# Value projection of the second row block: f32r parts replaced by scaled f16 high and low parts, with a new order of its banks

## The chip, the cores and the metric

The kernel runs on one core of one Trainium2 chip, in one launch. The metric is device microseconds of that core. The kernel before took 448.49 us, the median of three runs (447.81 to 448.59).

## What is computed

One layer of a hybrid bidirectional encoder over 1024 tokens of width 1024, in float32. A combined projection gives the queries, keys, values and gates of two head groups; group A attends in a 2-D neighbourhood of a 16 x 64 token grid, group B in a band of 128 tokens with rotary positions and a sink logit; each output is multiplied by SiLU of its gate, projected, added to the scaled input and normalised.

```python
h = jnp.einsum('bsd,de->bse', x, w_in[layer])
q_a, k_a, v_a, z_a, q_b, k_b, v_b, z_b = jnp.split(h, SPLIT_POINTS, axis=-1)
y_a = neighborhood_attention(q_a..., k_a..., v_a..., rel_pos_bias[layer])
y_b = windowed_gqa_with_sink(rotary(q_b), rotary(k_b), v_b..., sink_logits[layer])
mixed = jnp.concatenate([y_a * jax.nn.silu(z_a), y_b * jax.nn.silu(z_b)], axis=-1)
x = layer_norm(DEEPNORM_ALPHA * x + jnp.einsum('bse,ed->bsd', mixed, w_out[layer]), ...)
```

The change lies in the part of the first line that gives the values v_a (512 columns) and v_b (128 columns), 640 columns of W_in together.

## The kernel before

Float32 accuracy is had from parts of lower precision: an operand is split into a high part and a low part (what is left), and three matmuls are added up in PSUM, high x high, low x high and high x low. The tokens are dealt with in two row blocks (`half` 0 and 1) of 512 tokens; the inner dimension of 1024 is cut into KT = 8 slices k of 128.

The kernel opens with the value projection (L434 to L606), whose instructions are in an order written out by hand (`manual_schedule`, L548): each engine runs its own instructions in program order, and waits only for data and for buffers.

**First row block** (L549 to L564). Eight PSUM banks hold four token tiles t of 128 times two column halves a of 320. `load_wv(k)` (L457) loads 128 x 640 of the weights to `wvraw` (three buffers), ACT casts the high part `wvh` (L467), DVE subtracts for the low part `wvl` (L470), both in f32r. `load_x(half, k)` (L445) does the same for 128 x 512 of x transposed, by way of `xraw` (four buffers), giving `xh` and `xl`. The loop over k runs two slices of loads ahead of the matmuls; per k, 24 matmuls (`v_mms`, L478, L483) of 320 columns, with x stationary, go round the eight banks. From k = 4 on (`X1AT`) two slices of the second block's x are loaded and split beside it. `x_max` (L490) takes the maximum of |x| of each of the 16 slices on DVE.

**What is queued behind it** (L565 to L573): on SP's queue, five weight tiles of the later projections (`w_load`), ten loads of x once more (`x2_load`, L516), mask, sink and rotary tables. ACT empties the eight banks to `v32` (`v_out`, L539).

**Second row block** (L581 to L604). Bank by bank, i = 0 to 7, each with its 24 matmuls over k. Threaded into it: the scale of x (`x_scale`, L504: PE transposes the row maxima, DVE makes the power-of-two scale `xsc`), the scans of the first four weight tiles on ACT (`w_scan`, L234), sums of those on DVE (`z_tree`, L239 to L241), the scales of the first two projections (`w_scale`, L243: a small matmul into a bank with tag t, L249, and five small DVE operations), and the f16 parts of x, both halves, for the later projections (`x16_part`, L521): high on ACT (L529), low on DVE (L534) or, for five of the 16, on POOL in two instructions (L531, L532). `w_split(m)` (L196) makes the f16 parts of a weight tile: high on ACT (L204), low on POOL (L209, L210), and asks SP for the tile five further on. `v_max` (L543) takes the maximum of each token tile's values.

**After it** the projections `project(name)` (L379) run in f16, 48 matmuls of 512 columns each at L402. `v_scale` (L610), 16 matmuls into the first of them, needs all eight maxima; `v_part` (L623) writes the values' f16 parts to DRAM. The remaining weight tiles come through `sum_load` (L639) into tiles of the pool `big`. From L1185 on attention units are threaded between the rest of the projections, and `final` (L1053) ends with the output projection and the normalisation.

PSUM has eight banks under three tags: pj (2), s (4), t (2). `bank(tag)` hands one out; a matmul into a bank waits until the one that had it has been read. Tiles with one tag in an SBUF pool share its buffers in the same way.

Of the kernel before, what the change touches and what calls it, by code (L numbers as in the profile page):

```python
# [17 lines left out]
HD = 64  # L18
# [48 lines left out]
def hybrid_block(ctx, tc, xT, x, wt, wv, wo, bias, sink, gain, lbias, cos, sin, bmask, out):  # L67
# [4 lines left out]
    big = ctx.enter_context(tc.tile_pool(name="big", bufs=8))  # L72
# [15 lines left out]
    def big_tile(name, shape=(128, 2, 512), dt=F32R):  # L88
        n = taken[0]
        taken[0] += 1  # L90
        tag = "big" if n < 8 or 16 <= n < 24 or n >= 32 + NS else "big2"
        return big.tile(list(shape), dt, tag=tag, name=name)

    xh, xl, x16h, x16l = {}, {}, {}, {}
    for half in range(2):
        for k in range(KT):
            t = big_tile(f"x{half}{k}")
            xh[half, k], xl[half, k] = t[:, 0, :], t[:, 1, :]
# [335 lines left out]
    with ExitStack() as vctx:  # L434
# [10 lines left out]
        def load_x(half, k, cuts=(0, 512)):  # L445
            raw = vp.tile([128, 512], F32, tag="xr", name="xraw", bufs=4)
            for q, a, b in zip((nc.scalar, nc.sync) if len(cuts) == 3 else (nc.sync,), cuts, cuts[1:]):
                q.dma_start(raw[:, a:b], xT[half, k, :, a:b])
                yield
            for a, b in zip(cuts, cuts[1:]):  # L450
                (nc.scalar.copy if len(cuts) == 2 else nc.vector.tensor_copy)(xh[half, k][:, a:b], raw[:, a:b])
                yield
            for a, b in zip(cuts, cuts[1:]):
                nc.vector.tensor_sub(xl[half, k][:, a:b], raw[:, a:b], xh[half, k][:, a:b].bitcast(F32))
                yield

        def load_wv(k, cuts=(0, 640)):  # L457
            raw = vp.tile([128, 640], F32, tag="wvr", name="wvraw", bufs=3)
# [3 lines left out]
            h = vw.tile([128, 640], F32R, name=f"wvh{k}")  # L462
            l = vw.tile([128, 640], F32R, name=f"wvl{k}")
# [14 lines left out]
        def v_mms(ps, t, a, k, passes=(0, 1, 2)):  # L478
            ts = slice(128 * (t % 4), 128 * (t % 4) + 128)
            cs = slice(320 * a, 320 * a + 320)  # L480
            for i in passes:
                lh, rh = ((xh, wvh), (xl, wvh), (xh, wvl))[i]
                nc.tensor.matmul(ps[:, :320], lh[t // 4, k][:, ts], rh[k][:, cs],  # L483
                                 start=(k == 0 and i == 0), stop=(k == KT - 1 and i == 2))

        AXX = mybir.AxisListType.X
        xm = const.tile([128, 16], F32, name="xm")
        gm = const.tile([128, 1], F32, name="gm")

        def x_max(half, k):  # L490
# [848 lines left out]
```

## Time and profile before

| | |
|---|---|
| median of three runs | 448.49 us |
| the profiled execution: its time, its span | 447.78 us, 446.0 us |
| mean granted clock of PE | 0.999 |
| busy in the span: PE, DVE, ACT, POOL | 439.2, 344.3, 303.9, 229.2 us |
| L483, value projection, first matmul to the first of L402 | 4.14 to 61.41 us |
| second row block of it, first matmul to the first of L402 | 32.89 to 61.41 us |

How the views read. A row of the timeline has the start in us from the span's start, the time from the start of the row's first instruction to the end of its last, the engine, the line, the operation, the tiles written and read, the shape, and the number of instructions; in brackets what the engine waited for. Matmuls overlap: the next one starts while the last one drains, so the spacing of starts is the time that one costs, not its own duration. A row of the groups has the line, engine, operation and shape, then busy time and the mean of one in ns, then the idle time before. A row of the windows has a stretch, its length, each engine's busy time and count of instructions, PE's granted clock, the busy share of the DMA engines and the rate in GB/s. "PE a <- b" in the list of waits is followed by the total in us, the number and the longest. The profile's 40 slices give the busy share in tenths.

### The profile page before, as it was taken

The numbers are of one execution on the slowest core, as the hardware profiler recorded it, in microseconds if no ns is written. First come the engines' busy times: TensorE is split into PE (matmuls) and PEld (weight loads), VectorE is DVE, ScalarE is ACT, GpSimd is POOL, SyncE is SP. The second block draws the span as 40 slices with busy tenths as digits, with TensorE's granted clock in tenths as the row PEclk, the third lists the DMA queues.
The fourth block names the chain that finished last, engine by engine and source line by source line (L and its number), as shares of the span: only waits on it lengthen the run. The fifth ranks groups of instructions, "written<-read, shape, count | busy, mean of one in ns | idle before, by whom it ended". The sixth has DMA issues, their size and how long they took to land.

```text
span 446.0 us, 9544 instructions
## 1 busy us (share of the span) xinstructions
PE 439.2 (98%) x3269; PEld 262.9 (59%) x3269; DVE 344.3 (77%) x857; ACT 303.9 (68%) x704; POOL 229.2 (51%) x244
## 2 busy tenths in 40 slices
PE   9999999999999999999999999999999999999994
PEld 8999974444445555565555655655555654444442
DVE  5787987929989797786898888897767746179954
ACT  5648649878488998798978978797876876002211
POOL 0003942564837748768507628666762555005740
PEclk9999999999999999999999999999999999999999
DMA  7898377977847889788889999999999988101721
GB/s 243 295 313 281 93 255 244 282 257 264 291 135 160 154 172 174 141 148 142 152 166 177 189 184 191 205 169 231 203 191 219 161 195 323 49 0 71 252 79 71
DMA packets 135136, 83.86 MB, mean 188 GB/s; under 512 B 101424, under 2 KB 113456, under 8 KB 134832
## 3 DMA queue, kind: packets, MB, share of 16 engines
q1 hardware_dynamic: 134656, 82.77, 76.9%
q8 instruction: 25, 0.41, 0.4%
q10 hardware_dynamic: 432, 0.49, 0.3%
q14 instruction: 23, 0.19, 0.2%
HBM read 52.83 MB, written 9.96 MB: 141 GB/s over the span
## 4 chain that ended last, share of the span: by engine, by line
PE 98%; DVE 0%; ACT 0%; issue 0%; ACTq 0%
PE ps_pj L402 49%; PE ps_s L1036 9%; PE ps_t L889 7%; PE ps_s L483 6%; PE ps_pj L1036 5%; PE ps_t L1036 5%; PE ps_s L824 4%; PE ps_s L825 4%; PE ps_pj L483 3%; PE ps_t L483 3%; PE ps_t L909 2%; PE ps_t L442 1%; PE ps_t L1118 0%; DVE xr L1113 0%; ACT xr L1122 0%
## 5 line engine op out<-in xcount | busy, mean ns | idle before, releaser
L402 PE MATMUL ps_pj<-xf,wh 128*128 128x512 f16 x672 | 202.7, 379 | 0.0
L402 PE MATMUL ps_pj<-xf,wl 128*128 128x512 f16 x336 | 127.4, 379 | 0.0
L402 PEld LDWEIGHTS <-wh 128*128 128x128 f16 x672 | 63.8, 98 | 60.1 <-issue 0.2
L850 ACT ACTIVATE ps_s<-sn,nm 128x385 f32<-128x385 f32 (+3 forms) x128 | 70.0, 547 | 29.4 <-DVE nm L834 28.4
L861 DVE SCALAR_TENSOR_TENSOR split<-ps_s,split 128x384 f16<-128x384 f32 (+2 forms) x128 | 65.5, 512 | 17.2 <-ACT split L860 16.3
L1036 PEld LDWEIGHTS <-m 128*128 128x128 f16 x408 | 38.7, 98 | 42.7
L860 ACT ACTIVATE split<-ps_s 128x384 f16<-128x384 f32 (+2 forms) x128 | 57.5, 449 | 2.4
L402 PEld LDWEIGHTS <-wl 128*128 128x128 f16 x336 | 32.8, 98 | 36.7
L834 DVE CUSTOM_DVE_ANT_0 sn<-ps_s,bias,sg 128x264 f32<-128x264 f32 (+1 forms) x64 | 35.2, 550 | 16.5 <-PE ps_s L825 6.0
L209 POOL TENSOR_SCALAR wr<-wr,wsc 128x512 f32<-128x512 f32 x26 | 21.7, 836 | 40.7 <-ACT wh L204 35.1
L1036 PE MATMUL ps_s<-wo,m 128*128 128x512 f16 (+1 forms) x192 | 42.0, 373 | 0.0
L834 DVE CUSTOM_DVE_ANT_0 sn<-ps_s,bm,nsk 128x384 f32<-128x384 f32 (+1 forms) x64 | 40.6, 635 | 1.5 <-PE ps_s L825 1.3
L796 POOL TENSOR_SCALAR bias<-bias,rsg 128x552 f32<-128x552 f32 (+1 forms) x24 | 18.6, 776 | 41.2 <-DMA bias<-in_bias 37.9
L824 PE MATMUL ps_s<-ks,qs 128*128 128x384 f16 (+4 forms) x128 | 39.3, 307 | 0.0
L825 PE MATMUL ps_s<-ks,qs 128*128 128x384 f16 (+4 forms) x128 | 39.2, 307 | 0.0
L889 PEld LDWEIGHTS <-tr 128*128 128x128 f16 (+1 forms) x1104 | 36.6, 98 | 2.2
L210 POOL TENSOR_TENSOR wl<-wr,wh 128x512 f16<-128x512 f32 x26 | 32.2, 1239 | 2.2
L1093 ACT ACTIVATE sd<-mv,eps 128x1 f32<-128x1 f32 x8 | 2.4, 295 | 44.7 <-DVE mv L1091 42.4
L1135 POOL TENSOR_TENSOR xr<-xr,gb 128x512 f32<-128x512 f32 x7 | 11.2, 1606 | 40.1 <-ACT xr L1132 40.1
L483 PE MATMUL ps_s<-wvh,x 128*128 128x320 f32 x128 | 29.6, 311 | 0.0
L316 POOL COPY ks<-ks 64x512 f16<-64x512 f16 x40 | 25.9, 660 | 4.7 <-DVE ks L286 1.8
L1036 PE MATMUL ps_pj<-wo,m 128*128 128x512 f16 (+1 forms) x120 | 25.2, 347 | 0.0
(187 smaller groups left out, 827.8 us busy)
## 6 DMA issues: line engine op xcount, KB each, us to landing
xraw<-in_xT SPq DMA_DIRECT2D x31, 256.0 KB, 4.3
ws<-in_wt SPq DMA_DIRECT2D x15, 512.0 KB, 5.4
wr<-in_wt SPq DMA_DIRECT2D x26, 256.0 KB, 3.1
bias<-in_bias SPq DMA_DIRECT2D x16, 276.0 KB, 3.6
wor<-in_wo SPq DMA_DIRECT2D x16, 256.0 KB, 3.6
xr<-in_x SPq DMA_DIRECT2D x8, 512.0 KB, 9.5
out<-xr SPq DMA_DIRECT2D x14, 256.0 KB, 2.1
bias<-in_bias SPq DMA_DIRECT2D x8, 368.0 KB, 3.9
```

The lines of the kernel that those rows point to most:

```text
L210: nc.gpsimd.tensor_sub(l, raw, h)
L316: nc.gpsimd.tensor_copy(t[o, sl], t[a, sl])
L402: nc.tensor.matmul(ps, a[:, k % 4, :], mv, start=(k == 0 and i == 0), stop=(k == KT - 1 and i == 2))
L483: nc.tensor.matmul(ps[:, :320], lh[t // 4, k][:, ts], rh[k][:, cs], start=(k == 0 and i == 0), stop=(k == KT - 1 and i == 2))
L824: nc.tensor.matmul(ps[:, :m], q, sl[0], start=True, stop=False)
L825: nc.tensor.matmul(ps[:, :m], q, sl[1], start=False, stop=True)
L834: nc.vector.tensor_tensor_reduce(sn[:, :m], ps[:, :m], bias_t, sg[:, c:c + 1], init, op0=ALU.add, op1=ALU.min, accum_out=nm)
L850: nc.scalar.activation(pt[:, :m], sn[:, :m], AF.Exp, bias=nm, scale=-1.0, accum_out=sm[:, k:k + 1])
L860: nc.scalar.activation(hl[:, :m, 0, :c], src, AF.Copy, scale=PSCALE)
L861: nc.vector.scalar_tensor_tensor(hl[:, :m, 1, :c], src, PSCALE, hl[:, :m, 0, :c], op0=ALU.mult, op1=ALU.subtract)
L889: nc.tensor.matmul(ps[:, HD * m:HD * m + HD], a, b_, start=(i == 0), stop=(i == len(mms) - 1))
L1036: nc.tensor.matmul(ps, lh[:, ts], rh[:, cs], start=(e == EO[0] and i == 0), stop=(e == EO[-1] and i == 2))
```

## The change

- The first row block stays in f32r. Its loads of weights get eight raw buffers in place of three, and the raw weights are kept. ACT scans each (`wv_scan`); the second block's x is loaded raw into tiles of its own (`x1`), at k = 5, with no f32r split. `x_max` now runs over the high parts of the first block's eight slices and over four raw pairs of the second block.
- Inside the first block's matmuls, behind bank 4 of k = 5, a small matmul (`wv_scale`) gives the scale `wvs` of the value weights, and ACT makes their f16 high parts (`wv_hi`). Behind bank 0 of k = 7 another (`x_turn`, a plain f32 matmul into a free part of a bank in use, in place of the transpose into a bank of its own) gives `xsc`, which DVE finishes in `x_scale`.
- Then DVE makes `x1_hi(6)`, `x1_hi(7)`, the eight `wv_lo` and the eight `x1_lo`; ACT makes `x1_hi(0)` to `x1_hi(5)` with the emptying of the banks between them, the four scans and the eight `x2_hi`. The f16 parts of the second block's x are the ones that the later projections use, so x is loaded a second time only for the first block (8 loads, not 16); POOL makes three of its eight low parts.
- The second row block runs in f16: the four banks of column half 0 together, pass by pass (high x high over all k, then high x low of the weights, then low of x x high), then the four banks of column half 1 one after another in the order t = 2, 0, 1, 3, each over k with its three passes. `w_scale(0)`, `w_scale(1)` and the first two `w_split` move into these. `v_out` multiplies the second block's values by `vo`, which undoes the scales.
- The pools' tags follow: 16 tiles of 4 KB in `big` as before, now in four groups; `v32` takes over the buffers of `wvh`, the f16 weights those of `wvl` (two have their own), and `vt` those of the raw weights.

```diff
...
+SCALE_AT = ((5, 4), (7, 0))
...
-X1AT = 4
+X2POOL = (1, 3, 5)
...
-    big = ctx.enter_context(tc.tile_pool(name="big", bufs=8))
+    big = ctx.enter_context(tc.tile_pool(name="big", bufs=4))
...
+    xh, xl, x1, x1pair, x16h, x16l = {}, {}, {}, [], {}, {}
+    for k in range(KT):
+        t = big.tile([128, 2, 512], F32R, tag="xa" if k < 4 else "xb", name=f"x0{k}")
+        xh[k], xl[k] = t[:, 0, :], t[:, 1, :]
+    for k in range(0, KT, 2):
+        t = big.tile([128, 2, 512], F32, tag="xc", name=f"x1{k}")
+        x1[k], x1[k + 1] = t[:, 0, :], t[:, 1, :]
+        x1pair.append(t.rearrange("p i c -> p (i c)"))
...
-            raw = vp.tile([128, 640], F32, tag="wvr", name="wvraw", bufs=3)
+            raw = vp.tile([128, 640], F32, tag="wvr", name="wvraw", bufs=8)
+            wvr.append(raw)
...
+            h = vw.tile([128, 640], F32R, tag=f"vh{k}", name=f"wvh{k}")
+            l = vw.tile([128, 640], F32R, tag=f"vl{k}", name=f"wvl{k}")
...
-        def x_scale():
-            ps = bank("t")
-            nc.tensor.transpose(ps[:, :128], gm.to_broadcast([128, 128]), identf)
-            nc.vector.tensor_reduce(gm, ps[:, :128], axis=AXX, op=ALU.max)
+        vo = const.tile([128, 1], F32, name="vo")
+        wvs = const.tile([128, 1], F32, name="wvs")
+        wv16h, wv16l = {}, {}
+
+        def wv_scan(k):
+            nc.scalar.activation(scrap[:, :640], wvr[k], AF.Abs, accum_out=wvm[:, k:k + 1])
+
+        xm = const.tile([128, 12], F32, name="xm")
+
+        def x_max(i, src):
+            nc.vector.tensor_reduce(xm[:, i:i + 1], src, axis=AXX, op=ALU.max, apply_absolute_value=True)
+
+        def wv_scale(ps):
+            nc.tensor.matmul(ps[:, 320:328], ones, wvm.bitcast(BF16)[:, 1:2 * KT:2], start=False, stop=True,
+                             skip_group_check=True)
+            nc.vector.tensor_reduce(vo, ps[:, 320:328], axis=AXX, op=ALU.max)
+            nc.vector.tensor_scalar_max(vo, vo, 2.0 ** -30)
+            nc.vector.tensor_scalar(vo.bitcast(I32), vo.bitcast(I32), 0x7F800000, None, op0=ALU.bitwise_and)
+            nc.vector.tensor_scalar(wvs.bitcast(I32), vo.bitcast(I32), 0x7F800000, None, op0=ALU.bitwise_xor)
+
+        def wv_hi(k):
+            tag = f"vl{k}" if k < 6 else f"vx{k}"
+            t = vw.tile([128, 2, 640], F16, tag=tag, name=f"wf{k}")
+            wv16h[k], wv16l[k] = t[:, 0, :], t[:, 1, :]
+            nc.scalar.activation(wv16h[k], wvr[k], AF.Copy, scale=wvs)
+
+        def wv_lo(k):
+            nc.vector.scalar_tensor_tensor(wv16l[k], wvr[k], wvs, wv16h[k], op0=ALU.mult, op1=ALU.subtract)
+
+        def x_turn(ps):
+            nc.tensor.matmul(ps[:, 320:448], gm.to_broadcast([128, 128]), identf, start=False, stop=True,
+                             skip_group_check=True)
+
+        def x_scale(ps):
+            nc.vector.tensor_reduce(gm, ps[:, 320:448], axis=AXX, op=ALU.max)
             nc.vector.tensor_scalar_max(gm, gm, 2.0 ** -16)
             nc.vector.tensor_scalar(xrs.bitcast(I32), gm.bitcast(I32), 0x7F800000, None, op0=ALU.bitwise_and)
             nc.vector.tensor_scalar_mul(xrs, xrs, 2.0 ** -14)
             nc.vector.reciprocal(xsc, xrs)
 
...
+        def x16_alloc(half, k):
             if k % 2 == 0:
-                t = big_tile(f"xf{half}{k}", (128, 2, 2, 512), F16)
+                t = big.tile([128, 2, 2, 512], F16, tag="xd" if half else "xa", name=f"xf{half}{k}")
                 for i in range(2):
                     x16h[half, k + i], x16l[half, k + i] = t[:, i, 0, :], t[:, i, 1, :]
-            h, l = x16h[half, k], x16l[half, k]
-            nc.scalar.activation(h, raw, AF.Copy, scale=xsc)
-            if k in (1, 3) or (half, k) == (0, 5):
+
+        def x1_hi(k):
+            if k < 6:
+                nc.scalar.activation(x16h[1, k], x1[k], AF.Copy, scale=xsc)
+            else:
+                nc.vector.tensor_scalar_mul(x16h[1, k], x1[k], xsc)
+
+        def x1_lo(k):
+            nc.vector.scalar_tensor_tensor(x16l[1, k], x1[k], xsc, x16h[1, k], op0=ALU.mult, op1=ALU.subtract)
+
+        x2raw = {}
+
+        def x2_load(k):
+            if k < 4:
+                x2raw[k] = vp.tile([128, 512], F32, tag="xr", name="xraw2", bufs=4)
+            else:
+                x2raw[k] = vp.tile([128, 640], F32, tag="wvr", name="xraw2", bufs=8)[:, :512]
+            nc.sync.dma_start(x2raw[k], xT[0, k])
+
+        def x2_hi(k):
+            x16_alloc(0, k)
+            nc.scalar.activation(x16h[0, k], x2raw[k], AF.Copy, scale=xsc)
...
+        def x2_lo(k):
+            raw, h, l = x2raw.pop(k), x16h[0, k], x16l[0, k]
+            if k in X2POOL:
                 nc.gpsimd.tensor_scalar(raw, raw, xsc, 1.0, op0=ALU.mult, op1=ALU.mult)
                 nc.gpsimd.tensor_sub(l, raw, h)
             else:
                 nc.vector.scalar_tensor_tensor(l, raw, xsc, h, op0=ALU.mult, op1=ALU.subtract)
...
+        v32 = {}
...
+            if t < 4:
+                nc.scalar.copy(v32[t][:, cs], ps[:, :320])
+            else:
+                nc.scalar.activation(v32[t][:, cs], ps[:, :320], AF.Copy, scale=vo)
...
-        tags = ("pj", "pj", "s", "s", "t", "t", "s", "s")
-        banks = [bank(t) for t in tags]
+        ROT = ("pj", "s", "t", "s")
+        banks = {(t, a): bank(ROT[t]) for a in range(2) for t in range(4)}
...
-        interleave(load_wv(1), load_x(0, 1))
+        wv_scan(0)
+
+        def ahead(k):
+            interleave(load_wv(k), load_x(k))
+            wv_scan(k)
+            if k > 1:
+                x_max(k - 2, xh[k - 2].bitcast(F32))
+
+        ahead(1)
         for k in range(KT):
             if k + 2 < KT:
-                interleave(load_wv(k + 2), load_x(0, k + 2))
-            if k >= X1AT:
-                interleave(load_x(1, 2 * (k - X1AT)))
-                interleave(load_x(1, 2 * (k - X1AT) + 1))
-                x_max(0, k - X1AT)
+                ahead(k + 2)
+            if k + 3 == KT:
+                for j in range(KT):
+                    nc.sync.dma_start(x1[j], xT[1, j])
+                for j in (6, 7):
+                    x_max(j, xh[j].bitcast(F32))
+                x_max(8, x1pair[0])
             for ps in ([0], [1], [2]) if k == 0 else ([0, 1, 2],):
-                for a in range(2):
-                    for t in range(4):
-                        v_mms(banks[2 * t + a], t, a, k, ps)
+                for g in range(8):
+                    a, t = divmod(g, 4)
+                    for i in ps:
+                        lh, rh = ((xh, wvh), (xl, wvh), (xh, wvl))[i]
+                        nc.tensor.matmul(banks[t, a][:, :320], lh[k][:, 128 * t:128 * t + 128],
+                                         rh[k][:, 320 * a:320 * a + 320],
+                                         start=(k == 0 and i == 0), stop=(k == KT - 1 and i == 2))
+                    if (k, g) == SCALE_AT[0]:
+                        wv_scale(banks[t, a])
+                        for j in range(KT):
+                            wv_hi(j)
+                        for j in range(1, 4):
+                            x_max(8 + j, x1pair[j])
+                        nc.vector.tensor_reduce(gm, xm, axis=AXX, op=ALU.max)
+                    if (k, g) == SCALE_AT[1]:
+                        x_turn(banks[t, a])
+                        x_scale(banks[t, a])
+                        nc.vector.tensor_scalar(vo, vo, xrs, 0.5, op0=ALU.mult, op1=ALU.mult)
         for m in range(5):
             w_load(m)
-        for j in range(10):
-            x2_load(j)
+        for k in range(4):
+            x2_load(k)
         nc.sync.dma_start(bm, bmask)
         nc.sync.dma_start(sk, sink)
         for nm, src, tag in (("cos", cos, "zc"), ("sin", sin, "zs")):
             tiles[nm] = zslot(nm, tag)
             nc.sync.dma_start(tiles[nm], src)
-        for i in range(8):
-            v_out(banks[i], i // 2, i % 2)
+        for k in range(KT):
+            x16_alloc(1, k)
+        x1_hi(6)
+        x1_hi(7)
+        for k in range(KT):
+            wv_lo(k)
+        x1_hi(0)
+        v_out(banks[0, 0], 0, 0)
+        v_out(banks[1, 0], 1, 0)
+        x1_hi(1)
+        v_out(banks[2, 0], 2, 0)
+        v_out(banks[3, 0], 3, 0)
+        for k in range(2, 6):
+            x1_hi(k)
+        for t in range(4):
+            v_out(banks[t, 1], t, 1)
+        for k in range(KT):
+            x1_lo(k)
         for k in range(4, KT):
-            x_max(0, k)
+            x2_load(k)
+        for m in range(4):
+            w_scan(m)
+        for n in range(2):
+            z_tree(n)
         for k in range(KT):
-            x_max(1, k)
-        nc.vector.tensor_reduce(gm, xm, axis=AXX, op=ALU.max)
-        for i in range(8):
-            if i in (0, 1):
-                w_scan(2 * i)
-                w_scan(2 * i + 1)
-            if i == 5:
-                nc.vector.tensor_scalar_mul(nsk, sk, -1.0)
-            ps = bank(tags[i])
+            x2_hi(k)
+        for k in X2POOL:
+            x2_lo(k)
+
+        def v16(ps, t, a, k, i):
+            lh, rh = ((x16h, wv16h), (x16h, wv16l), (x16l, wv16h))[i]
+            nc.tensor.matmul(ps[:, :320], lh[1, k][:, 128 * t:128 * t + 128], rh[k][:, 320 * a:320 * a + 320],
+                             start=(k == 0 and i == 0), stop=(k == KT - 1 and i == (2 if a == 0 else 2)))
+
+        set_a = [bank(r) for r in ROT]
+        for i in range(3):
             for k in range(KT):
-                v_mms(ps, 4 + i // 2, i % 2, k)
-                if i == 1 and k == 2:
-                    x_scale()
-                if i in (1, 2) and k == 4:
-                    z_tree(i - 1)
-                if i in (2, 3) and k == 4:
-                    w_scale(i - 2)
-            if 1 <= i < 5:
-                for j in range(4 * (i - 1), 4 * (i - 1) + 4):
-                    x16_part(j)
-                    x2_load(j + 10)
-            v_out(ps, 4 + i // 2, i % 2)
-            if i >= 3:
-                v_max(i - 3)
-            if i in (3, 4):
-                w_split(i - 3)
-        for t in range(5, 8):
-            v_max(t)
+                for t in range(4):
+                    v16(set_a[t], t, 0, k, i)
+        for t in range(4):
+            v_out(set_a[t], 4 + t, 0)
+        for k in (0, 2):
+            x2_lo(k)
+        set_b = [bank(r) for r in ROT]
+        for n, t in enumerate((2, 0, 1, 3)):
+            for k in range(KT):
+                for i in range(3):
+                    v16(set_b[t], t, 1, k, i)
+                if (n, k) == (0, 6):
+                    w_scale(0)
+                    w_split(0)
+                    w_split(1)
+                    x2_lo(4)
+                    x2_lo(6)
+                    x2_lo(7)
+                if (n, k) == (1, 5):
+                    w_scale(1)
+                    nc.vector.tensor_scalar_mul(nsk, sk, -1.0)
+                    for j in range(4):
+                        v_max(j)
+            v_out(set_b[t], 4 + t, 1)
+            v_max(4 + t)
...
-                vt = vp.tile([128, 10, 2, HD], F16, tag=("vt", "wvr")[t % 2], name=f"vt{t}", bufs=3)
+                vt = vp.tile([128, 10, 2, HD], F16, tag="wvr", name=f"vt{t}", bufs=8)
```

More of the change, by code (lines that the diff above doesn't have):

```diff
@@ L86, in hybrid_block, with big_tile @@
     taken = [0]
-    def big_tile(name, shape=(128, 2, 512), dt=F32R):
+    def big_tile(name, shape, dt):
         n = taken[0]
         taken[0] += 1
[L91 to L98, printed above, removed]
+        return big.tile(list(shape), dt, tag="xb" if n % 8 < 4 else "xc", name=name)
+    xh, xl, x1, x1pair, x16h, x16l = {}, {}, {}, [], {}, {}
[6 more added lines that the diff above has]
+        x1pair.append(t.rearrange("p i c -> p (i c)"))
     zt = {}
@@ L476, in interleave @@
                 gens = [g for g in gens if next(g, g) is not g]
[L478 to L484, printed above, removed]
         AXX = mybir.AxisListType.X
-        xm = const.tile([128, 16], F32, name="xm")
```

38 lines of the change are left out of this document (9 added, 29 removed).

## Prediction

> **What bounds the kernel now.** I read the page's first lines and its chain of work first, then the list of PE's waits, then the timeline of PE, DVE, ACT and POOL from 13 to 72 us, where the value projection lies.
>
> ```profile
> span 446.0 us, 9544 instructions
> ...
> PE   9999999999999999999999999999999999999994
> ...
> PEclk9999999999999999999999999999999999999999
> DMA  7898377977847889788889999999999988101721
> ...
> PE 98%; DVE 0%; ACT 0%; issue 0%; ACTq 0%
> ```
>
> The chain that ended last is PE from end to end, the clock is granted in full, and PE is busy in every slice. The list of PE's waits, whole, says the same:
>
> ```profile
> PE ps_t L1118 <- ACT dg L1117: 1.5, 1, 1.5
> PE ps_t L442 <- DVE warm L439: 1.0, 1, 1.0
> ```
>
> One wait lies ahead of the first matmul and one behind the last projection. In between PE waits for nothing, so a microsecond of matmul time taken out of the value projection is a microsecond of the span, and a new wait of PE costs the same. The other engines matter only where PE comes to wait for them.
>
> The second row block is the stretch that the change rewrites:
>
> ```profile
> 32.89 0.46 PE L483 MATMUL ps_pj<-wvh,x 128*128 128x320 f32 x2
> ...
> 61.41 0.61 PE L402 MATMUL ps_pj<-xf,wh 128*128 128x512 f16 x2
> 61.86 0.38 PE L402 MATMUL ps_pj<-xf,wl 128*128 128x512 f16 x1
> 62.07 0.59 PE L402 MATMUL ps_pj<-xf,wh 128*128 128x512 f16 x2
> 62.50 0.38 PE L402 MATMUL ps_pj<-xf,wl 128*128 128x512 f16 x1
> 62.72 0.59 PE L402 MATMUL ps_pj<-xf,wh 128*128 128x512 f16 x2
> ...
> 437.19 1.50 PE L1036 MATMUL ps_pj<-wo,m 128*128 128x128 f16 x24
> ...
> L483 PEld LDWEIGHTS ps_s<-wvh,x 128*128 128x128 f32 x128 | 21.7, 189 | 0.0
> L402 PEld LDWEIGHTS <-wh 128*128 128x128 f16 x672 | 63.8, 98 | 60.1 <-issue 0.2
> ```
>
> It runs from 32.89 to 61.41, 28.52 us for 192 matmuls of 320 columns and three small ones (L506, twice L249). At about 0.1 us for each of those, my estimate, one f32r matmul comes every 0.147 us. In f16, four matmuls of 512 columns take 61.86 to 62.72, 0.215 each, and 24 of 128 columns take 1.50, less the last one's tail of 0.22, 0.056 each. 320 columns lie halfway between: 0.1355. The weight loads point to the reason: 189 ns each in f32r and back to back, 98 ns in f16, well below a matmul.
>
> **The change part by part.**
>
> *Matmuls.* 192 x (0.147 - 0.1355) = **2.2 us less**; the block would take 26.0 us of issue. [...]
>
> *Scales found in the first block.* Two small matmuls enter PE's queue there. For their time I take the first block as it stands: PE passes the place (5, 4) at 24.53 and (7, 0) at 29.81.
>
> ```profile
> 24.53 0.45 PE L483 MATMUL ps_s<-wvh,x 128*128 128x320 f32 x2
> 29.81 0.45 PE L483 MATMUL ps_s<-wvh,x 128*128 128x320 f32 x2
> 440.93 0.91 PE L1118 MATMUL ps_t<-xr,dg 128*128 128x384 f32 x2 [1.53 <-ACT dg L1117]
> ...
> 28.42 7.79 DVE L492 TENSOR_REDUCE xm<-x 128x1 f32<-128x512 f32 x13
> 36.24 0.17 DVE L580 TENSOR_REDUCE gm<-xm 128x1 f32<-128x16 f32 x1
> 38.03 0.29 DVE L507 TENSOR_REDUCE gm<-ps_t 128x1 f32<-128x128 f32 x1 [1.62 <-PE ps_t L506]
> 38.93 0.16 DVE L511 RECIPROCAL xsc<-xrs 128x1 f32<-128x1 f32 x1
> ...
> L662 DVE TENSOR_REDUCE wm<-ws 128x1 f32<-128x1024 f32 x2 | 2.4, 1208 | 0.0
> ...
> 0.00:10.00 10.00, 8.92 (x63) 8.47 (x64) 5.17 (x12) 5.50 (x9) 0.70 (x6) 1.00 0.81 251
> 10.00:20.00 10.00, 10.00 (x71) 10.00 (x70) 7.30 (x11) 6.63 (x11) 0.00 (x0) 1.00 0.85 283
> ```
>
> The first one (8 columns) costs some 0.04. It needs the eight new scans of the raw weights on ACT; these take over the ACT and DVE time of the removed f32r split of the second block's x (8 casts, 8 subtractions), and PE is there three loads later, so this is covered. DVE then does four small operations; L507 to L511 are five in 1.06, so wvs is there at about 25.6. Three maxima over 1024 elements follow, 1.13 each back to back (1.21 less the 0.08 by which L492's thirteen overlap), and one of 0.17: gm at 29.2, 0.6 ahead of PE. The second matmul is plain f32 where L506 was a transpose. L1118, f32 with 384 columns, shows two records in 0.91; 128 columns lie between 0.056, the f16 matmul of that width, and 0.9, and I take 0.3, a third of L1118, as it is the like operation. Its five DVE operations end 1.06 after it: xsc at 31.3. The first block ends at 32.89 + 0.34 = **33.2**.
>
> The eight x1 loads no longer wait for raw buffers, but stand in one row on SP's queue behind x7, ahead of five w loads, four x2 loads, the masks and the rotary tables. To the last x1 byte 6.8 MB are moved; at 251 and 283 GB/s, the rates of the first two windows, that is 25.4 us, while the last maximum starts at 27.9. Eight x2 loads (2 MB) drop out altogether; the wv loads no longer wait for buffers. Neither has PE behind it.
>
> *High parts on ACT, pass 0.*
>
> ```profile
> 69.15 1.54 ACT L634 ACTIVATE vt<-v,vrs 128x640 f16<-128x640 f32 x2
> ...
> 39.12 2.56 ACT L529 ACTIVATE xf<-xraw,xsc 128x512 f16<-128x512 f32 x4 [0.86 <-DVE xsc L511]
> 41.59 0.41 ACT L541 COPY v<-ps_pj 128x320 f32<-128x320 f32 x1
> ...
> 36.93 0.63 ACT L234 ACTIVATE junk<-wr 128x512 bf16<-128x512 f32 x1
> ...
> 37.56 0.62 ACT L234 ACTIVATE junk<-wr 128x512 bf16<-128x512 f32 x1
> ```
>
> Eight wv_hi at 0.72 (L634: 1.54 for two, one alone 0.82) run from 25.6 to 31.4, just when xsc comes. x1_hi costs 0.615 (L529), v_out 0.31 to the next start, 0.41 to its own end. In program order: x1_hi(0), two v_out, x1_hi(1), two v_out, done at 33.9; x1_hi(2) to (5) at 34.5, 35.1, 35.8, 36.4. PE wants the fourth bank at 33.6 and then a new k every 4 x 0.1355 = 0.54, a little faster than ACT makes them; k = 6 and 7 come from DVE. Pass 0 ends at 38.0 and not at 33.2 + 4.35 = 37.55: **0.45 us of waiting**.
>
> *Low parts on DVE, passes 1 and 2.* This is where the change can fail, since DVE's low parts read two SBUF operands and POOL works beside them.
>
> ```profile
> 39.01 0.41 DVE L239 TENSOR_TENSOR junk<-junk 128x512 bf16<-128x512 bf16 x1
> 39.92 0.74 DVE L534 SCALAR_TENSOR_TENSOR xf<-xraw,xsc,xf 128x512 f16<-128x512 f32 x1
> 46.00 4.13 DVE L534 SCALAR_TENSOR_TENSOR xf<-xraw,xsc,xf 128x512 f16<-128x512 f32 x3
> ...
> L1120 DVE SCALAR_TENSOR_TENSOR xr<-xr,rstd,bb 128x640 f32<-128x640 f32 x1 | 0.9, 884 | 0.0
> ...
> L451 DVE CAST x<-xraw 128x256 fp32r<-128x256 f32 x2 | 0.6, 294 | 3.1 <-DMA xraw<-in_xT 3.1
> ...
> 44.97 0.69 POOL L531 TENSOR_SCALAR xraw<-xraw,xsc 128x512 f32<-128x512 f32 x1
> 45.74 1.17 POOL L532 TENSOR_TENSOR xf<-xraw,xf 128x512 f16<-128x512 f32 x1
> 46.89 1.14 POOL L531 TENSOR_SCALAR xraw<-xraw,xsc 128x512 f32<-128x512 f32 x1
> 48.11 1.48 POOL L532 TENSOR_TENSOR xf<-xraw,xf 128x512 f16<-128x512 f32 x1
> ```
>
> Alone a low part of 512 takes 0.74 (0.665 to the next start), one of 640 0.88 (0.80). Beside POOL three take 4.13: they and POOL's instructions end in turn, DVE 0.55 after POOL, POOL 0.57 or 1.03 after DVE. Each POOL instruction between two low parts so adds 0.45 or 0.91.
>
> From xsc at 31.3 DVE has one small operation (0.2), x1_hi(6) and (7), eight wv_lo, eight x1_lo. No row has DVE scale 512 elements from SBUF: its cast of 256 in 0.294 gives some 0.42 for 512, the low part's rate 0.67; I take 0.42, as the cast is the like operation. wv_lo ends at 31.5 + 0.85 + 6.4 = 38.8; pass 1 wants its last part at 41.8, so that is covered. x1_lo would end at 44.1 alone. POOL begins when ACT has written x2_hi(1): 36.3 + 4 x 0.31 + 4 x 0.625 (w_scan) + 2 x 0.615, some 41.6 with the hand-over. By then DVE is in x1_lo(4), so three POOL instructions fall ahead of x1_lo(7): 44.1 + 1.9 = 46.0. Pass 2 begins at 42.35 and wants x1_lo(7) at 46.1. **Covered, by 0.1.** The first four banks end at 46.7.
>
> *The second four banks.* z_tree(0) has POOL's other three instructions between its steps and ends at 49.1; w_scale(0) wants it on PE at 46.7 + 21 x 0.1355 = 49.55. DVE goes on with z_tree(1) (0.9, as L239 to L534's start) and two low parts (1.3) to 51.2, then reads w_scale(0)'s bank by 51.5. PE comes to w_scale(1) at 52.4 and takes a t bank; the one that w_scale(0) used is free. wh(0), wh(1), the remaining low parts and the maxima end by about 61.9, while the first project matmuls are met by parts done at 58 and v_scale asks for its maximum 16 matmuls (3.4 us) after the block.
>
> *Sum.* 33.2 + 0.45 + 26.0 + 0.1 = 59.75 against 61.41: 1.65 us less. The covers of 0.1 and 0.4 are thinner than the error of the terms ahead of them, and I take off 0.25: **1.4 us less**. The profiled execution took 447.78 (span 446.0 and 1.78 around it), so 446.4 on its time; it lies 0.71 below the median of the runs, 448.49, from which 1.4 gives **447.1**. Bounds of the unseen costs: the plain f32 matmul at 0.056 or 0.9 moves the end by -0.25 or +0.6, x1_hi on DVE at 0.67 by +0.4 (the cover of pass 2 is gone), at 0.29, the cast of half the length, by nothing. Forecast alone: 446.3 to 447.8.
>
> **The rivals.**
>
> *The t bank.* If the two t banks are handed out strictly in turn, w_scale(1) gets that of the first bank of the second four, which ACT empties only behind wh(0) and wh(1): wsc at 52.1, two parts of 0.625, v_out 0.41, 53.8. PE waits 1.4 us and the gain is 0.2: 448.3. In the program of the kernel before, the 71 t tiles alternate save at one place, where one bank comes twice running, which speaks for the order of release and against this; nothing in the profile tells.
>
> *Later transfers.* The page's slices have the DMA engines at 0.9 and more through the middle. If transposed tiles come no earlier, attention matmuls wait and the gain goes there: 448.5. Against it: not one wait of PE for a DMA in the list above.
>
> *No gain in f16 at 320 columns.* If the spacing stayed at 0.147, the block would take 28.2 and end at 62.0: 449.0. For it nothing but that no row has 320 columns in f16; against it the f16 rows of 128 and 512, both near 0.42 ns a column. [...]
>
> *Slower: x1 lands late.* PE stands in order behind the matmul that turns gm, so a late last x1 tile stops the first block itself. With the landing at L, gm is there at L + 1.4, and PE waits L + 1.4 - 29.85; from L = 30.1 on the 1.65 us are gone. At 200 GB/s behind the first window's 2.5 MB, L is 31.5, PE waits 3.05, and the time is 449.9. For it: eight x1 loads and nine others now stand on one queue at once. Against it: the rates shown, taken while loads waited for buffers.
>
> **How the numbers follow.** What a measurement of this kernel can tell from no change is 0.2%, 0.9 us. Forecast 0.54, of which 0.50 lies more than that below the median; bank 0.16, later transfers 0.08, f16 0.05, all within; late x1 0.17, of which 0.16 above. Faster 0.50, same 0.34, slower 0.16. The range 446.2 to 449.6 takes in all cases but the far part of the last.
>
> **What would show it.** Right: matmuls of the second block 0.135 apart; ACT's x1_hi pacing pass 0; low parts of 1.1 to 1.6 us beside POOL; no PE wait at w_scale(0) and (1); the first project matmul near 60. Wrong: a PE wait for gm near 30 us, for a low part in pass 2 of over 0.5, or for v_out ahead of w_scale(1); or the first project matmul early and new PE waits behind it.

## The result, and the profile after

The changed kernel takes **447.07 us**, the median of nine runs (446.49 to 447.43), against 448.49 for nine of the kernel before beside them: a ratio of 0.9968, 95% interval 0.9957 to 0.9978, or 1.42 us less. Taken again later on one chip with 12 runs it was 447.25 against 448.48, ratio 0.9969 (0.9956 to 0.9983). The profiled execution took 447.43, with a span of 445.6.

The page of the kernel after, its first line, one of its 40-slice rows and its chain, by engine and by line:

```profile
span 445.6 us, 9522 instructions
...
PE   9999999999999999999999999999999999999994
...
PE 88%; DMA 6%; ACT 3%; DVE 1%; issue 0%; SPq 0%; ACTq 0%; DVEq 0%
PE ps_pj L405 47%; PE ps_s L1122 9%; PE ps_t L975 7%; PE ps_pj L1122 5%; PE ps_t L1122 5%; PE ps_s L910 4%; PE ps_s L911 4%; PE ps_s L662 3%; PE ps_t L995 2%; PE ps_t L662 1%; DMA wos<-in_wo 1%; PE ps_pj L662 1%; DMA wr<-in_wt 1%; DMA x<-in_xT 1%; ACT wf L511 1%; DMA wvraw<-in_wv 1%
```

PE is still busy in every slice. But the chain that ended last is no longer PE alone: 6% of the span goes to DMA and 3% to ACT. Followed in order of time, most of this lies ahead of 34 us: loads (18.9 of DMA's 25.6 us), then ACT's `wv_hi` (L511), up to a copy of L571 for which PE waits. One transfer, of a tile `wos` of the output weights (6.7 us from 115.16), stands in the middle of the run, so there too PE now stands behind something late; more of that below. First the value projection, from PE's timeline after the change (start, length, line, shape, count), with the last row of the kernel's matmuls:

```profile
25.14 0.30 PE L608 MATMUL ps_pj<-wvl,x 128*128 128x320 f32 x1
25.29 0.18 PE L500 MATMUL ps_pj<-wvm,ones 128*128 128x8 bf16 x1
...
30.69 0.38 PE L517 MATMUL ps_pj<-identf,gm 128*128 128x128 f32 x2
...
33.99 0.31 PE L662 MATMUL ps_pj<-wf,xf 128*128 128x320 f16 x1
34.14 0.30 PE L662 MATMUL ps_s<-wf,xf 128*128 128x320 f16 x1
34.55 0.30 PE L662 MATMUL ps_t<-wf,xf 128*128 128x320 f16 x1
34.87 0.30 PE L662 MATMUL ps_s<-wf,xf 128*128 128x320 f16 x1
...
38.97 0.30 PE L662 MATMUL ps_pj<-wf,xf 128*128 128x320 f16 x1
...
55.79 5.19 PE L662 MATMUL ps_s<-wf,xf 128*128 128x320 f16 x37
60.81 0.59 PE L405 MATMUL ps_pj<-xf,wh 128*128 128x512 f16 x2
...
440.59 0.91 PE L1204 MATMUL ps_t<-xr,dg 128*128 128x384 f32 x2 [1.53 <-ACT dg L1203]
```

- The second row block runs from 33.99 to 60.81, **26.82 us where it was 28.52: 1.70 less**. In the row at 55.79, 37 f16 matmuls, the rest of the block, take 60.81 - 55.79 = 5.02, 0.1357 each; f32r took 0.147.
- Pass 0, the first 32 matmuls, takes 33.99 to 38.97, 4.98 where 32 x 0.1357 = 4.34 would do: **0.64 of waiting**, most of it the steps of 0.41 and 0.32 ahead of its third and fourth matmul.
- The first block ends 1.10 later than before (33.99 for 32.89). From the matmul ahead of place (5, 4), at 25.14 here and 0.147 ahead of 24.53 before, to the block's end it is 8.85 and 8.51 us: **the two small matmuls cost 0.34**. The other 0.76 had been lost ahead of them, in the first slice k, where PE's matmuls came 0.27 us apart in place of 0.147 until the trace's record of the full clock begins, at 5.0 us before and at 6.7 after. Over the 13 profiles of this study it began anywhere from 3.7 to 9.9 us, and the first slice took 3.9 to 6.1 us, so profiles can differ by some 2 us in it with no part of the change behind it.

Without that start the sum is -1.70 + 0.34 = -1.36. From the start of the first project matmul to that of the last matmul of all (at 441.02 after, 441.35 before), however, it is 380.21 us after and 379.94 before, 0.27 given back. What made the parts, in the timelines of ACT, DVE and POOL after:

```profile
26.35 5.87 ACT L511 ACTIVATE wf<-wvraw,wvs 128x640 f16<-128x640 f32 x8 [6.83 <-DVE wvs L505]
32.20 0.72 ACT L535 ACTIVATE xf<-x,xsc 128x512 f16<-128x512 f32 x1
...
34.07 0.42 ACT L571 COPY v<-ps_t 128x320 f32<-128x320 f32 x1
34.38 0.45 ACT L571 COPY v<-ps_s 128x320 f32<-128x320 f32 x1
34.69 2.58 ACT L535 ACTIVATE xf<-x,xsc 128x512 f16<-128x512 f32 x4
```

```profile
32.20 0.88 DVE L537 TENSOR_SCALAR xf<-x,xsc 128x512 f16<-128x512 f32 x2
32.99 6.45 DVE L514 SCALAR_TENSOR_TENSOR wf<-wvraw,wvs,wf 128x640 f16<-128x640 f32 x8
39.36 5.38 DVE L540 SCALAR_TENSOR_TENSOR xf<-x,xsc,xf 128x512 f16<-128x512 f32 x8
44.66 0.41 DVE L242 TENSOR_TENSOR junk<-junk 128x512 bf16<-128x512 bf16 x1
45.11 0.67 DVE L243 TENSOR_TENSOR junk<-junk 128x256 bf16<-128x256 bf16 x1
...
51.73 0.28 DVE L255 TENSOR_REDUCE wg<-ps_t 128x1 f32<-128x128 f32 x1
```

```profile
42.33 3.31 POOL L558 TENSOR_SCALAR xraw<-xraw,xsc 128x512 f32<-128x512 f32 x1 [41.03 <-ACT xf L553]
45.73 1.16 POOL L559 TENSOR_TENSOR xf<-xraw,xf 128x512 f16<-128x512 f32 x1
```

PE's third and fourth bank stand behind the two copies of L571 at 34.07 and 34.38. DVE's 16 low parts run from 32.99 to 44.74 without a break. POOL's first instruction, ready at 42.33, takes 3.31 us where its like took 0.69 before: it gets in only beside L243, whose 0.29 became 0.67.

### The profile page after: what moved, and what is told of

It is laid out like the page before. It is cut to its first block, busy times and chain, and to the rows that moved or that the text cites. A ratio compares the mean times of both kernels' runs of the same rounds, so it can differ in the third digit from the quotient of the medians.

```text
span 445.6 us, 9522 instructions
## 1 busy us (share of the span) xinstructions
PE 438.6 (98%) x3271; PEld 254.3 (57%) x3271; DVE 345.7 (78%) x862; ACT 309.0 (69%) x718; POOL 227.0 (51%) x240
## 4 chain that ended last, share of the span: by engine, by line
PE 88%; DMA 6%; ACT 3%; DVE 1%; issue 0%; SPq 0%; ACTq 0%; DVEq 0%
PE ps_pj L405 47%; PE ps_s L1122 9%; PE ps_t L975 7%; PE ps_pj L1122 5%; PE ps_t L1122 5%; PE ps_s L910 4%; PE ps_s L911 4%; PE ps_s L662 3%; PE ps_t L995 2%; PE ps_t L662 1%; DMA wos<-in_wo 1%; PE ps_pj L662 1%; DMA wr<-in_wt 1%; DMA x<-in_xT 1%; ACT wf L511 1%; DMA wvraw<-in_wv 1%
## 5 line engine op out<-in xcount | busy, mean ns | idle before, releaser
L920 DVE CUSTOM_DVE_ANT_0 sn<-ps_s,bm,nsk 128x384 f32<-128x384 f32 (+1 forms) x64 | 40.7, 636 | 1.8 <-PE ps_s L911 1.3
L882 POOL TENSOR_SCALAR bias<-bias,rsg 128x552 f32<-128x552 f32 (+1 forms) x24 | 18.7, 779 | 40.3 <-DMA bias<-in_bias 32.0
L558 POOL TENSOR_SCALAR xraw<-xraw,xsc 128x512 f32<-128x512 f32 x3 | 4.9, 1645 | 41.0 <-ACT xf L553 41.0
```

The source lines that it names most:

```text
L920: nc.vector.tensor_tensor_reduce(sn[:, :m], ps[:, :m], bias_t, sg[:, c:c + 1], init, op0=ALU.add, op1=ALU.min, accum_out=nm)
```

## The experiments

**The order of the first four banks.** In the second row block the first four banks go one after another over k with their three passes, like the last four.

```diff
-        for i in range(3):
+        for t in range(4):
             for k in range(KT):
-                for t in range(4):
+                for i in range(3):
                     v16(set_a[t], t, 0, k, i)
```

> The first four banks of the second row block are taken one after another, each over k with its three passes, as the last four are; all else as in the changed kernel. Theory (the order by passes hides the low parts behind the high ones): in the changed kernel's profile x1_lo(0) ends at 40.1 us and x1_lo(7) at 44.7 while PE is ready at 34.0, so the first bank ends near 44.9 and three more at 3.26 each make the set end near 54.7 instead of 47.7: 7.0 us more, about 454; up to 1.7 more if PE's clock falls in the pause. Rival (the order is free, only the f16 spacing counts): 447.1, no wait.

It took 455.22. A row of the list of PE's waits, and then the windows (start and end, length, busy time and count of PE, PEld, DVE, ACT and POOL, granted clock, DMA share, rate):

```profile
PE ps_pj L662 <- DVE xf L540: 5.7, 1, 5.7
```

```profile
38.00:39.50 1.50, 0.00 (x0) 0.00 (x0) 1.50 (x3) 1.50 (x6) 0.00 (x0) 0.78 0.47 178
39.50:46.30 6.80, 5.96 (x25) 3.46 (x26) 6.73 (x12) 6.72 (x15) 3.73 (x2) 0.55 0.00 1
46.30:50.00 3.70, 3.70 (x29) 2.65 (x28) 3.63 (x6) 0.89 (x2) 3.62 (x4) 1.00 0.00 0
```

PE waits 5.7 us for x1_lo(0), which a bank by bank order needs at once; and in that pause, which lasts to 40.3, the granted clock falls: it is halved from 38.84 on, for 6.8 us, and full again in the last of these windows. The second block is 7.9 us longer. For the clock I had put up to 1.7 us, an estimate that no run gave; here 18 matmuls from 40.34 on take 4.98, 0.27 apart in place of 0.136. So the passes are what covers the low parts.

**The f32r spacing.** In the kernel before, the second block's matmuls are cut to 256 of their 320 columns (the last 64 of each column half are not computed).

```diff
-                nc.tensor.matmul(ps[:, :320], lh[t // 4, k][:, ts], rh[k][:, cs],
+                n = 320 if t < 4 or (k == 0 and i == 0) else 256
+                nc.tensor.matmul(ps[:, :n], lh[t // 4, k][:, ts], rh[k][:, 320 * a:320 * a + n],
```

> The kernel before, with the second row block's f32r matmuls at 256 columns instead of 320 (all but the first of each bank): the last 64 value columns of each half get only their first product. Theory (an f32r matmul comes every 0.147 us because of its weight load, which does not shrink): spacing stays 0.147, the block 28.5 us, the time 448.5. Rival (it is the columns, streamed more slowly in f32r): spacing 0.118, the block 5.4 us shorter, 443.1.

```profile
33.88 0.40 PE L484 MATMUL ps_pj<-wvh,x 128*128 128x256 f32 x2
34.11 0.28 PE L484 MATMUL ps_pj<-wvl,x 128*128 128x256 f32 x1
34.23 0.40 PE L484 MATMUL ps_pj<-wvh,x 128*128 128x256 f32 x2
34.46 0.28 PE L484 MATMUL ps_pj<-wvl,x 128*128 128x256 f32 x1
34.58 0.40 PE L484 MATMUL ps_pj<-wvh,x 128*128 128x256 f32 x2
```

From 33.88 to 34.58 six matmuls pass, 0.117 each; 320 columns took 0.147, and 0.117 / 256 and 0.147 / 320 are both 0.46 ns a column. My reason for the f32r spacing, the weight loads, falls: the columns themselves stream more slowly, 0.46 ns against 0.42 in f16. (The time, 446.69, where this rival had 443.1, holds 3.1 us of PE's waits that are new in this kernel.)

**The x1 tiles late.** The eight x1 loads go behind the five w loads, the x2 loads and the tables on SP's queue.

```diff
             if k + 3 == KT:
+                for m in range(5):
+                    w_load(m)
+                for j in range(4):
+                    x2_load(j)
...
                 for j in range(KT):
                     nc.sync.dma_start(x1[j], xT[1, j])
```

> The second row block's raw tiles (1 MB) are put behind the first five projection tiles, four raw tiles of the third use, the masks, the sink and the rotary tables on SP's queue, so that they land late; nothing else moves. My account says that the gain hangs on these tiles landing before the scales are due: gm has to be there at 30.8 us (the first block's turn matmul stands behind k7), and the tiles land at about 22.7 now. By the queue's share (some 3 MB ahead, 300 GB/s, 10 us) the last would land at 32 to 34 us, gm some 1 us behind it, the f16 parts behind that: TensorE should stop at the turn matmul by 3 to 5 us, the kernel should take 450 to 452.5, and the wait should be listed at that matmul with gm as its releaser. The rival, that the tiles are not what the scales wait for (the scan of wv, ended at 19.5, or the chain on VectorE sets them), gives 447.1.

It took 453.21, a little above the 450 to 452.5 expected. Its waits of PE:

```profile
PE ps_pj L517 <- DVE gm L626: 1.8, 1, 1.8
...
PE ps_pj L617 <- DVE vo L502: 1.0, 1, 1.0
...
PE ps_t L662 <- ACT v L571: 0.6, 1, 0.6
```

The rival "x1 lands late" is a real mechanism: PE stops at the matmul that turns gm, 1.8 us, less than the 3 to 5 expected there. For there is a wait that I had not named: `wvs` (L502 to L505) stands on DVE behind the first maximum of an x1 pair, so that PE stops 1.0 us already for that. First block (without its first k) and pass 0 together are 3.3 + 0.5 = 3.8 us longer; the rest of the 5.8 us between the two profiles is a late start of the full clock (1.2, and 0.4 to the first matmul) and 0.3 behind the first project matmul.

**Who keeps whom out.** One low part, x1_lo(1), goes to POOL, ready in the middle of DVE's run.

```diff
-            nc.vector.scalar_tensor_tensor(x16l[1, k], x1[k], xsc, x16h[1, k], op0=ALU.mult, op1=ALU.subtract)
+            if k == 1:
+                nc.gpsimd.tensor_scalar(x1[k], x1[k], xsc, 1.0, op0=ALU.mult, op1=ALU.mult)
+                nc.gpsimd.tensor_sub(x16l[1, k], x1[k], x16h[1, k])
...
```

> One low part of the second row block, x1_lo(1), goes from VectorE to GpSimd, whose first of its two instructions is ready at about 34.5 us, in the middle of VectorE's unbroken run of low parts (33.0 to 44.7 us). Theory from the profile after the change: an unbroken run of VectorE's two-operand f32 instructions keeps GpSimd out until it ends; then GpSimd's instruction would show some 9 to 10 us (0.69 alone), end at about 44.7, its second part at about 46, and pass 2, whose k = 1 is due at 43.9, would wait about 2 us: 449. The rival is the prediction's own step, that the two engines take turns: GpSimd is done by about 37.5 us, VectorE's run gets about 1 to 1.5 us longer, nothing waits, 447.1.

It took 447.25, and POOL and DVE show:

```profile
34.34 1.67 POOL L541 TENSOR_SCALAR x<-x,xsc 128x512 f32<-128x512 f32 x1 [33.04 <-ACT xf L535]
36.10 1.60 POOL L542 TENSOR_TENSOR xf<-x,xf 128x512 f16<-128x512 f32 x1
42.40 1.50 POOL L562 TENSOR_SCALAR xraw<-xraw,xsc 128x512 f32<-128x512 f32 x1 [4.70 <-ACT xf L557]
...
33.06 7.71 DVE L514 SCALAR_TENSOR_TENSOR wf<-wvraw,wvs,wf 128x640 f16<-128x640 f32 x8
40.70 6.41 DVE L544 SCALAR_TENSOR_TENSOR xf<-x,xsc,xf 128x512 f16<-128x512 f32 x7
```

My theory of the changed kernel's profile falls. Alone POOL's instruction takes 0.69; at 34.34 it waited 0.98 more and at 42.40 0.81 more, about the rest of the low part that ran and one further of 0.66 to 0.80, and then it was in. The one at 42.40 is the very instruction that took 3.31 in the changed kernel at 42.33. DVE's run was stretched by 1.3 us to 40.7 and ended at 47.1, and no wait of PE followed, though x1_lo(7) was there only 0.1 ahead of PE: pass 2 begins at 43.4 in this profile and wants it 28 matmuls later, at 47.2. What decides between turns and being kept out stays open: the 3.31 came back as 3.31 to 3.32 in four other profiles with DVE's work unchanged, so it is not chance from run to run.

**Without POOL.** All x2 low parts go to DVE (`X2POOL` empty, with k = 1, 3, 5 ahead of 0 and 2).

```diff
-        for k in X2POOL:
+        for k in (1, 3, 5):
             x2_lo(k)
```

> The three low parts of the third use's tiles that GpSimd makes go to VectorE, behind the two z trees. If contention between the two engines costs the time nothing, as TensorE's unbroken passes say, the time stays at 447.1 within 0.3, the z trees take about 2 us in place of 4.4, and the scale wsc is written at about 52.2 us in place of 52.6. The rival: three instructions of 0.69 more on VectorE make the first projection's scale late, which would be a wait of up to 2 us in front of its first matmuls at 60.8, 449.

447.32, the second block 26.82 as it was.

```profile
46.13 3.40 DVE L561 SCALAR_TENSOR_TENSOR xf<-xraw,xsc,xf 128x512 f16<-128x512 f32 x5
50.38 0.29 DVE L255 TENSOR_REDUCE wg<-ps_t 128x1 f32<-128x128 f32 x1 [0.86 <-PE ps_t L252]
```

DVE takes three instructions more and still reads w_scale(0)'s bank at 50.38, 1.35 earlier than at 51.73 and now waiting for PE. As far as this one run shows, the contention costs the engines time and the kernel nothing.

**One t bank.** w_scale(1) goes into the first bank of the second four, as the rival had it.

```diff
-                    w_scale(1)
+                    w_scale(1, set_b[2])
```

> w_scale(1) writes into the bank that the first of the last four banks used, in place of a t bank handed out to it; all else as in the changed kernel. Theory (the t bank matters, the wait is for v_out behind two weight parts on ACT): in the changed kernel's profile that v_out ends at 54.36 and PE is at the place at 53.42, so PE waits 0.95 us: 448.0. The prediction's rival had 1.4: 448.5. Rival (the wait is absorbed, since PE has other work): 447.1.

447.40, ratio to before 0.9977 (0.9961 to 0.9993): it can't be told from the changed kernel, where 0.95 more was expected. ACT and PE of this kernel:

```profile
51.68 1.34 ACT L207 ACTIVATE wh<-wr,wsc 128x512 f16<-128x512 f32 x2 [2.42 <-DVE wsc L258]
52.92 0.51 ACT L573 ACTIVATE v<-ps_t,vo 128x320 f32<-128x320 f32 x1
...
53.48 0.22 PE L252 MATMUL ps_t<-cs,ones 128*128 128x128 bf16 x1
```

The order is the rival's, wh(0), wh(1), then the bank (free at 53.43), and PE comes to it at 53.48. The price is gone because wsc came 0.9 us earlier than in the changed kernel's profile: beside POOL two low parts of L561 took 1.75 here and 2.77 there. The rival's price hangs on which of the two engines goes first.

**Earlier loads and scales.** The loads run three slices ahead and the two scales are taken at (4, 4) and (6, 4).

```diff
-SCALE_AT = ((5, 4), (7, 0))
+SCALE_AT = ((4, 4), (6, 4))
...
         ahead(1)
+        ahead(2)
         for k in range(KT):
-            if k + 2 < KT:
-                ahead(k + 2)
-            if k + 3 == KT:
+            if k + 3 < KT:
+                ahead(k + 3)
+            if k + 4 == KT:
```

> Loads run three slices ahead of PE instead of two, and the two scale matmuls stand at (4, 4) and (6, 4) instead of (5, 4) and (7, 0). Theory (pass 0 waits 0.46 us for ACT, whose high parts come late because the scales come late): the wait is gone, pass 0 takes 4.35 to 4.45 us instead of 4.98, and the time is 446.6. Rival (pass 0 is paced by ACT's 0.615 per high part against PE's 0.54 wherever the scales stand): 447.0. Rival (x1 lands too late for (6, 4)): PE waits for gm there, 447.1 or more.

446.42, ratio 0.9945 (0.9925 to 0.9965). Pass 0 takes 4.36 and no longer waits; the second block takes 26.20. But from the first project matmul to the last matmul it is 380.67, 0.73 more than before.

**What gives it back.** ACT, DVE and PE at 122 us, first in the changed kernel and then in the one before:

```profile
121.91 0.63 ACT L434 ACTIVATE scrap<-wos 128x512 bf16<-128x512 f32 x1 [4.01 <-DMA wos<-in_wo]
...
122.54 0.67 ACT L365 ACTIVATE z<-ps_pj,invt 128x512 f32<-128x512 f32 x1
...
123.24 0.69 DVE L366 SCALAR_TENSOR_TENSOR z<-z,ps_pj 128x512 f32<-128x512 f32 x1 [0.29 <-ACT z L365]
...
123.59 0.27 PE L911 MATMUL ps_s<-ks,qs 128*128 128x256 f16 x1
123.98 0.59 PE L405 MATMUL ps_pj<-xf,wh 128*128 128x512 f16 x2
```

```profile
122.15 0.63 ACT L431 ACTIVATE scrap<-wos 128x512 bf16<-128x512 f32 x1 [3.64 <-DMA wos<-in_wo]
...
123.58 0.69 DVE L363 SCALAR_TENSOR_TENSOR z<-z,ps_pj 128x512 f32<-128x512 f32 x1
...
124.21 0.27 PE L825 MATMUL ps_s<-ks,qs 128*128 128x256 f16 x1
124.32 0.59 PE L402 MATMUL ps_pj<-xf,wh 128*128 128x512 f16 x2
```

ACT scans a tile of the output weights that has not landed, and behind it stands the tanh of a gate (L365), whose bank DVE empties (L366) and PE wants next. Before, ACT's wait ended while DVE was still busy. Now all the work is 0.6 us earlier and the transfer only 0.24, and PE loses 0.28: 123.59 to 123.98 is 0.39, where the same step was 0.11 before. The other profiles with the scan in its old place, the one with the earlier loads among them, bear this out: where ACT waited 2.7 to 3.0 us for the tile PE lost nothing, and waits of 4.01, 4.09, 4.18, 4.48 and 4.78 cost PE 0.28, 0.35, 0.45, 0.74 and 1.06, each time about what lay above 3.73. The scan goes behind, four steps into the next stage:

```diff
-PRE_AT = (12, 20)
+PRE_AT = (4, 12, 20)
```

Alone, and with the earlier loads:

> The same move of that one scan in the changed kernel without the earlier loads. Theory: the change gave back 0.28 us of its gain at 123.6 us because everything ahead of the scan came earlier while its transfer did not; with the scan moved the time falls from 447.1 to 446.8. The rival: no difference, 447.1, if the gap of 0.28 us comes from VectorE's row of instructions and not from ScalarE's wait.

> The kernel with the earlier loads and scales (446.42, its pass 0 without a wait), in which one instruction group more is moved: the fourth of ScalarE's early scans of the output weights, which waits 4.5 us for its transfer at 117 to 121.7 us with the read of a projection bank behind it, goes behind the stage's start, four steps into the next stage. Theory: the 0.73 us that TensorE loses at 123 us is that scan, and nothing else stands there, so from the first projection on the kernel is as long as before the change (379.9) and the time falls to 445.7. The rival: the same work waits a little later on something else (the bank's other readers, the transfer itself), and the time stays at 446.4.

Alone 447.01 (ratio 0.9973, 0.9963 to 0.9982), with the earlier loads 446.06 (0.9954, 0.9941 to 0.9966). In both profiles PE's wait is gone and the stretch from the first project matmul is 379.95 and 379.93 us, as before the change. (Two profiles with the scan in its old place had 379.94 as well, those where ACT waited 2.7 and 3.0.) The times follow less clearly: the first can't be told from no difference, the second lies 0.36 above the number expected. So the changed kernel and the version with both were set side by side on one chip:

> The changed kernel once more, as it is, beside the version with the earlier loads and the moved scan, on one chip: the profiles' marks without the start of the clock say that the two differ by 0.62 (the wait in pass 0) plus 0.27 (the gap at 123.6 us). Expected: 447.1, some 0.9 above the other. The rival, that the executions' spread in the first 10 us covers any difference: within 0.4 of the other.

> Earlier loads and the moved scan together, beside the changed kernel on one chip: expected 446.1, 0.9 under it; by the rival within 0.4 of it.

447.25 and **445.99**, ratios 0.9969 (0.9956 to 0.9983) and 0.9938 (0.9924 to 0.9952): 1.26 us apart, and the intervals don't meet. That is more than the 0.9 expected. A possible reason stands in the list of waits of the one execution of the changed kernel that was profiled here:

```profile
PE ps_pj L405 <- DVE z L366: 0.9, 1, 0.9
```

The same place as the 0.28; the gap in PE's starts is 1.06 here, and the transfer landed later still (ACT waits 4.78 for it, where it was 4.01). In the profiles with the scan in its old place and the changed kernel's loads the gap was 0 to 1.06; how large it was in the other eleven executions isn't known, so the difference of the medians is not shown to come from it.

## Why the prediction was right, and where it was not

The forecast was 1.4 us less, and 1.42 was measured. The main terms came much as they stood there, but that the sum agrees to the hundredth is luck: its parts agree less well.

- *Matmuls, 2.2 less.* Right: 0.147 to 0.1357 is 2.17 for 192. The rival "no gain in f16" is out. The weight loads as the reason did not hold up.
- *Two small matmuls, 0.34.* Right to the hundredth, by luck, since it is split otherwise: about 0.13 and 0.22 by the starts around L500 and L517, where 0.04, an estimate that no row gave, and 0.3 had been put.
- *x1 and gm, PE not stopped.* Right: no wait at L517. That it would stop with late tiles, the late loads showed (1.8 us). The wait for vo is one that the prediction left out.
- *Pass 0, 0.45.* The mechanism is right, ACT's high parts with copies between them, the size 0.64. It showed earlier than said, at the third and fourth bank, and taking the scales earlier removed all of it.
- *Low parts beside POOL.* **This is the step that failed**: "By then DVE is in x1_lo(4), so three POOL instructions fall ahead of x1_lo(7): 44.1 + 1.9 = 46.0." It ended at 44.74, none of POOL's ahead of it. Pass 2 begins at 33.99 + 4.98 + 4.35 = 43.32 and wants it 28 matmuls later, at 47.1: its cover, said to be 0.1, was 2.4, and the 0.25 taken off for thin covers had nothing to pay for there. Turns were the wrong model for that start of POOL, and right for the one in the run with x1_lo(1), where the cover, with one low part fewer on DVE, came to 0.1. Why POOL was kept out in the one and not in the other stays open.
- *t bank.* In the changed kernel w_scale(1) found a free bank; with the one bank forced PE lost 0.03, for the reason above. So the 1.4 was not shown.
- *Later transfers.* This rival came true for a fraction, by another road: not transposed tiles but a weight tile on its way to ACT, 0.28 in one profile, 1.06 in another. The sum had put it at nothing, and the rival was given a small chance, from a list of waits in which DVE's own work hid it.

So the 0.25 came near the truth for another reason than the one given: without it the sum was 1.65, and what the profile takes from that is 0.19 more in pass 0, some 0.1 of small differences, and 0.27 given back behind the projection. Together the profile gives -1.70 + 0.34 + 0.27 = -1.09 without the start of the clock, and the two medians -1.42 and -1.23; -1.09 lies in the interval of the ratio (-1.9 to -1.0), so the last three tenths can't be assigned.

## What to carry to other kernels

A kernel whose bounding engine never waits can still be one late transfer from a wait: look behind the engine that does wait for a DMA (here ACT, 3.6 us, some 0.1 short of costing PE time, because DVE was as late), for what moves earlier with the change and what doesn't. Passes over all k across several banks buy the time in which low parts are made; the same matmuls in bank order cost 7.9 us, 5.7 of it in one wait. Where two engines contend, price both orders.

## What the runs showed of the hardware that was not expected

- f32r matmuls cost 0.46 ns a column at 256 and 320 columns, f16 0.42.
- The same GpSimd instruction in the same run of VectorE's two-operand instructions took 3.31 us in five profiles and 1.50 in another kernel's, where 0.69 is its time alone. At the end of an instruction of VectorE it was not always the next: by the starts, four more passed it in the 3.31 (three low parts and L242) and one in the 1.50.
- The full clock at the start of the kernel came anywhere from 3.7 to 9.9 us in 13 profiles: at 5.0 in that of the kernel before, at 6.7 in that of the changed kernel.
- Ahead of the full clock f32r matmuls of 320 columns came 0.27 us apart, and f16 ones at half clock (the run in bank order, 18 in 4.98 us) 0.27 as well: the f32r penalty of 0.147 against 0.136 showed at the full clock alone.
